# Turns between the stages of a two-layer streaming trunk, put in another order

## The chip, the core and the metric

One core of a Trainium2 chip runs the kernel. The metric is device microseconds (us) of one execution; three timed executions and one with the profiler stand below. TensorE (PE) multiplies, VectorE (DVE), ScalarE (ACT) and GpSimd (POOL) work on tiles of 128 partitions, and SyncE (SP) issues DMA transfers. TensorE runs at one of two levels, 2.4 or 1.2 GHz; the profile gives the granted clock as a share of the higher one.

## The reference, cut to what matters

Two layers on 1024 prompt rows and 128 sample rows, model width D = 1024, inner width E = 2048, all in float32.

```python
# mixer A: gated MLP over chunks of 128 rows
uv = gelu((xn @ w_in)[:, :2*E]); u, v = uv[:, :E], uv[:, E:]; z = (xn @ w_in)[:, 2*E:]
s = causal_mix(w_s, layernorm(v)) + b_s
x = x + (u * s * silu(z)) @ w_out
# mixer B: xLSTM memory, 4 heads of 512
xm, z = split(rmsnorm(x) @ b_w_in)            # each 2048 wide
xc = silu(causal_conv(xm))                    # 4 taps
q, k, v = blockdiag(xc, wq), blockdiag(xc, wk), blockdiag(xm, wv)
ig, fg = split(concat(q, k, v) @ w_gates + b_gates); lf = log_sigmoid(fg)
# running sums and maxima of ig, lf along the rows give weights exp(...)
C = decay * C + sum(w * k v^T);  h = (q C, intra-chunk part) / normaliser
x = x + ((layernorm(h) + skip * xc) * silu(z)) @ b_w_out
y = rmsnorm(x)                                # and C, n, m, conv of both row groups
```

## The kernel before, in words

**Numbers.** A float32 operand is split into a high part (ACT, a copy with rounding, line L89) and a low part (DVE, a subtraction, L90). A product is three matmuls into one PSUM sum: high by high, high by low, low by high (`mm3`). So before PE can start on an operand, ACT and then DVE have worked on it. PE's program order is the order of the code (class `Ordered`, L49); the order on the other engines is set by the framework's planner when the kernel is built, from its own estimate of times. SP's queue issues in order: an entry that waits holds up all behind it.

**Stages.** The 1152 rows are nine row tiles of 128, taken as three blocks of 384 (b). Mixer A first makes v, then a loop over 16 blocks of 128 features (f, L463 to L531) makes u, z and their product. It works on four quarters of 288 rows with seven products; their sums come out of PSUM by copies and additions (L499, L515 to L527, on tiles `c1`, `U2`, `e5`, `t`, `uq`), and two quarters each of `uq` and `c1` are written to o_d in DRAM, one step later, by the list `late` (L483).

The out-projection of A (L640 to L676) runs c (two halves of the output columns) by b by f: it loads a tile of o_d (`or`, L656), splits it (`os`) and multiplies. After each c and b `half_out` (L620) adds the residual and stores x1; with c = 1 it also sums squares on ACT (L632), and computes the normalised rows `xs` on DVE (L638), with the norm's weights `gB` (loaded at L594). `enter(n)` transposes row tile n on PE and splits it into `xh`, `xl`; most of these stand inside the next block, those of tiles 6 to 8 in mixer B's first steps (L832).

Mixer B's steps t (L820 to L843) make xm for a feature block and row block, the convolution, values, keys, and gate partials; q, k, v go to DRAM. Then 48 z blocks follow, each 24 matmuls of 128 by 384 with a Silu on ACT (L858) and a store (L859). `z_to(k)` (L865) emits z blocks until k are done. It is called between the parts of the gate stage (L885 to L1000): gate rows copied from PSUM (`rA`, L887), 48 small matmuls that add up the gate rows, then on tiles of 4 partitions by 1152 an Exp, a Ln, scans and three more Exps, and PE transposes of the results (`tpk`). After it the z blocks carry the state work by a plan (L1413 ff.): streams of 512 KB pieces of C in and out. Heads and the last projection follow.

Of the kernel before, what the change touches and what calls it, by code (L numbers as in the profile page):

```python
# [70 lines left out]
def trunk_kernel(ctx: ExitStack, tc: tile.TileContext, ins: dict, outs: list):  # L71
# [392 lines left out]
    for f in range(NF):  # L464
# [17 lines left out]
        def rows_of(o, q):  # L482
            late.append(lambda f=f: S.dma_start(out=o_d[f * P:(f + 1) * P, quarter(q)], in_=o))  # L483

        for i in range(7):
            rows_out_, late = late, []
            for p in range(2):
# [22 lines left out]
                elif i in (4, 5):  # L510
                    z, q = (e5[p], q1) if i == 4 else (U2[p], q0)
                    V.tensor_tensor(out=z, in0=acc, in1=z, op=ALU.add)
                    t = az.tile([P, QT], F32, name="t", bufs=3)
                    A.activation(out=t, in_=z, func=AF.Tanh, scale=0.5)
# [78 lines left out]
    wsm3 = kp_.tile([P, 3, NF, 4], F32, name="wsm3")  # L593
    gB = load_gB(ins["norm_g"][1], kp_, "gB")  # L594

# [24 lines left out]
    def half_out(n, c, po):  # L620
# [3 lines left out]
        S.dma_start(out=xv, in_=rows(n, ins["x_prompt"], ins["x_sample"])[:, cs])  # L624
        V.tensor_tensor(out=xv, in0=xv, in1=po, op=ALU.add)
        A.dma_start(out=x1_d[n][:, cs], in_=xv)
        if c == 0:
# [11 lines left out]
        xs_[n] = xs  # L639

    for c in range(2):
        for b in range(NB):
            po = [ps.tile([P, DH], F32, name="sm") for _ in range(3)]
            for f in range(NF):
# [7 lines left out]
                if c == 1 and b == 0 and f < 2:  # L652
                    fetch_wo(1, NF - 2 + f)
                    split_wo(1, NF - 2 + f)
                raw = ow.tile([P, BT], F32, name="or", bufs=6)
                S.dma_start(out=raw, in_=o_d[f * P:(f + 1) * P, b * BT:(b + 1) * BT])  # L656
                o = ow.tile([P, 2, BT], F32R, name="os")
# [9 lines left out]
            if c == 1 and b == 2:  # L667
                ow_stack.close()
                A_stack.close()
                rawp = ctx.enter_context(tc.tile_pool(name="rawp", bufs=4))  # L670
                wp = ctx.enter_context(tc.tile_pool(name="wp", bufs=6))
                w_first = load_w(b_w[:, :, 0:P])
            for j in range(3):
# [153 lines left out]
    for t, (f, b) in enumerate(steps):  # L827
        ft = feats[f]
        ft.inputs(b)
        if b == 0:  # L830
            ft.gate_weights()
        if (f, b) in ((1, 0), (1, 1)):  # L832
            for n in ((6,), (7, 8))[b]:
                enter(n)
        for j, part in ((t - 1, Feature.values), (t - 2, Feature.keys)):
            if j >= 0:
                part(feats[steps[j][0]], steps[j][1])
        if b == 1:
            ft.history()
        if t == 4 or (f > 1 and b == 1):  # L840
            if len(feats) < NF:
                feats.append(Feature(len(feats)))
            else:  # L843
                z_weights(0)
# [41 lines left out]
    for b in range(NB):  # L886
        V.tensor_copy(out=gsb[:, b * BT:(b + 1) * BT], in_=gp[32 * b:32 * b + 8])  # L887
    z_to(2)

# [23 lines left out]
    A.activation(out=t3, in_=t2, func=AF.Ln)  # L913
    z_to(4)
    lf = gt.tile([H, NTK], F32, name="rF")
# [5 lines left out]
    V.scalar_tensor_tensor(out=lf, in0=fg, scalar=0.0, in1=t3, op0=ALU.min, op1=ALU.subtract)  # L921
    z_to(6)

# [11 lines left out]

    z_to(7)

# [23 lines left out]
    V.tensor_tensor(out=cc_, in0=bb, in1=mt, op=ALU.subtract)  # L961
    z_to(8)
    wi_ = gt.tile([H, NTK], F32, name="rC")
# [12 lines left out]
    G.tensor_scalar(out=mt, in0=mt, scalar1=1e30, scalar2=1e-30, op0=ALU.min, op1=ALU.max)  # L976
    z_to(10)

# [430 lines left out]

    z_to(11)  # L1410
    open_head()
    z_to(12)
    heads[0].queries()  # L1413
    plan = {}
    plan.setdefault(13, []).append(heads[0].keys)
    plan.setdefault(14, []).append(heads[0].normaliser)
    first, rate = 14, (3 * NF - ZEND - 14) / (ZDEC - 1)
    for j in range(ZDEC):
# [169 lines left out]
```

## Time and profile before

| | |
|---|---|
| median of three timed runs | 1970.63 us (1969.28 to 1977.24) |
| profiled execution | 1961.52 us |
| its span on the core | 1959.8 us |
| mean granted clock of PE | 0.986 |
| PE busy | 1900.5 us, 11553 matmuls |
| DVE busy | 1270.3 us |
| ACT busy | 850.0 us |
| POOL busy | 621.4 us |

Busy times are of the span. PE is the engine that is almost always busy, so a time off the kernel must come from a stretch in which PE stands, or runs at the lower clock. Where the timeline says `[6.61 <-ACT os L89]`, the engine stood 6.61 us before this instruction, and what came last was the instruction named. PEclk in a window is 1.00 for the higher level throughout and 0.50 for the lower.

### The profile page before, as it was taken

The numbers are of one execution on the slowest core, as the hardware profiler recorded it, in microseconds if no ns is written. First come the engines' busy times: TensorE is split into PE (matmuls) and PEld (weight loads), VectorE is DVE, ScalarE is ACT, GpSimd is POOL, SyncE is SP. The second block draws the span as 40 slices with busy tenths as digits, with TensorE's granted clock in tenths as the row PEclk, the third lists the DMA queues.
The fourth block names the chain that finished last, engine by engine and source line by source line (L and its number), as shares of the span: only waits on it lengthen the run. The fifth ranks groups of instructions, "written<-read, shape, count | busy, mean of one in ns | idle before, by whom it ended". The sixth has DMA issues, their size and how long they took to land.

```text
span 1959.8 us, 32037 instructions
## 1 busy us (share of the span) xinstructions
PE 1900.5 (97%) x11553; PEld 1681.2 (86%) x11553; DVE 1270.3 (65%) x2522; ACT 850.0 (43%) x1727; POOL 621.4 (32%) x637
## 2 busy tenths in 40 slices
PE   7999999999998999989999989999999999999998
PEld 6888999999998788889999959888987787788887
DVE  5822477777776354477667635222498798898897
ACT  5422444444444243455555635112343344344454
POOL 3000244444441000035444401000145435345466
PEclk9999999999999999999999979999999999999999
DMA  6222333333334654335555554687998897775533
GB/s 213 92 92 77 106 98 103 103 103 99 103 98 163 200 170 142 113 99 154 161 162 156 167 152 143 207 259 235 282 306 264 267 284 243 261 239 177 154 122 129
DMA packets 345690, 328.21 MB, mean 167 GB/s; under 512 B 28164, under 2 KB 276948, under 8 KB 345532
## 3 DMA queue, kind: packets, MB, share of 16 engines
q1 hardware_dynamic: 288812, 261.03, 43.3%
q10 hardware_dynamic: 56720, 65.13, 10.6%
q8 instruction: 91, 1.49, 0.3%
q14 instruction: 67, 0.55, 0.1%
HBM read 203.07 MB, written 123.02 MB: 166 GB/s over the span
## 4 chain that ended last, share of the span: by engine, by line
PE 74%; DVE 13%; DMA 7%; ACT 2%; issue 2%; POOL 1%; SPq 1%; ACTq 0%; POOLq 0%; DVEq 0%
PE sm L58 74%; DVE Cst L1278 2%; DMA cw<-cw_d 2%; DVE c L1129 2%; DVE Cl L90 1%; DVE qT L1252 1%; DMA out<-c 1%; DVE raw L1361 1%; DVE bst L1318 1%; DMA c<-in_state_mlstm_C 1%; DMA vv<-vb_d 1%; DMA r<-in_a_w_in 0%; DVE dn L1324 0%; DVE x L1380 0%; DMA st_d<-w 0%
## 5 line engine op out<-in xcount | busy, mean ns | idle before, releaser
L58 PE MATMUL sm<-xh,w 128*128 128x384 f32 x1536 | 410.9, 341 | 4.3 <-DVE w L90 1.5
L58 PEld LDWEIGHTS sm<-xh,w 128*128 128x128 f32 x1536 | 281.5, 189 | 12.8 <-issue 8.2
L58 PE MATMUL sm<-xl,w 128*128 128x384 f32 x768 | 260.4, 339 | 1.1 <-DVE xl L90 1.1
L58 PE MATMUL sm<-Xh,w 128*128 128x288 f32 x1024 | 216.3, 298 | 4.6 <-ACT c L499 4.6
L58 PE MATMUL sm<-w,o 128*128 128x512 f32 x864 | 209.9, 398 | 2.9 <-ACT o L89 1.2
L58 PE MATMUL sm<-w,os 128*128 128x512 f32 x864 | 200.7, 393 | 6.6 <-ACT os L89 6.6
L58 PEld LDWEIGHTS sm<-w,os 128*128 128x128 f32 x864 | 162.9, 190 | 42.8 <-ACT os L89 9.1
L58 PEld LDWEIGHTS sm<-w,o 128*128 128x128 f32 x864 | 159.8, 188 | 41.1 <-ACT hn L1330 1.7
L58 PE MATMUL sm<-w,Xh 128*128 128x512 f32 x576 | 180.2, 394 | 1.8 <-DVE w L90 1.4
L58 PEld LDWEIGHTS sm<-Xh,w 128*128 128x128 f32 x1024 | 168.2, 189 | 5.2 <-ACT c L499 5.0
L90 DVE TENSOR_TENSOR w<-r,w 128x512 fp32r<-128x512 f32 x176 | 136.1, 779 | 50.3 <-ACT w L89 49.8
L58 PE MATMUL sm<-S,w 128*128 128x288 f32 x1152 | 163.8, 297 | 0.0
L90 DVE TENSOR_TENSOR w<-raw,w 128x1024 fp32r<-128x1024 f32 x44 | 56.4, 1281 | 156.8 <-ACT w L89 156.7
L58 PEld LDWEIGHTS sm<-S,w 128*128 128x128 f32 x1152 | 155.1, 188 | 0.8
L58 PE MATMUL sm<-Xl,w 128*128 128x288 f32 x512 | 151.4, 296 | 0.0
L58 PEld LDWEIGHTS sm<-xl,w 128*128 128x128 f32 x768 | 145.1, 189 | 1.3 <-DVE xl L90 1.3
L89 ACT CAST w<-r 128x512 fp32r<-128x512 f32 x176 | 107.3, 618 | 68.8 <-PE sm L58 29.3
L58 PEld LDWEIGHTS sm<-w,Xh 128*128 128x128 f32 x576 | 108.0, 189 | 25.3 <-DVE w L90 2.6
L58 PE MATMUL sm<-w,Xl 128*128 128x512 f32 x288 | 112.6, 391 | 0.0
L90 DVE TENSOR_TENSOR os<-or,os 128x384 fp32r<-128x384 f32 x96 | 53.0, 556 | 90.1 <-ACT os L89 90.1
L58 PE MATMUL sm<-va,k 128*128 128x258 f32 (+1 forms) x768 | 104.5, 286 | 3.4 <-DVE x L1380 1.7
L89 ACT CAST w<-raw 128x1024 fp32r<-128x1024 f32 (+1 forms) x56 | 55.2, 987 | 116.6 <-DMA raw<-in_b_w_in 91.2
(306 smaller groups left out, 3734.5 us busy)
## 6 DMA issues: line engine op xcount, KB each, us to landing
c<-in_state_mlstm_C SPq DMA_DIRECT2D x64, 512.0 KB
out<-c SPq DMA_DIRECT2D x64, 512.0 KB
r<-in_a_w_in SPq DMA_DIRECT2D x96, 256.0 KB
or<-o_d SPq DMA_DIRECT2D x96, 192.0 KB
raw<-in_b_w_in SPq DMA_DIRECT2D x32, 512.0 KB
qT<-q_d SPq DMA_DIRECT2D x40, 256.0 KB
vh<-v_d SPq DMA_DIRECT2D x48, 192.0 KB
vb_d<-st ACTq DMA_DIRECT2D x48, 192.0 KB
```

The lines of the kernel that those rows point to most:

```text
L58: ins = fn(*args, **kw)
L89: first = A.copy(out=hi, in_=src)
L90: (lo_eng or V).tensor_tensor(out=lo, in0=src, in1=f32(hi), op=ALU.subtract)
L1129: V.scalar_tensor_tensor(out=c0[:, cc], in0=c0[:, cc], scalar=decB[:, d.h, 8 + b:9 + b], in1=pc, op0=ALU.mult, op1=ALU.add)
L1252: V.tensor_tensor(out=u.g["qT"], in0=u.g["qT"], in1=u.g["cw"][:, 1:2].to_broadcast([P, DC, P]), op=ALU.mult)
L1278: V.scalar_tensor_tensor(out=Cst[:, c, a, :w], in0=Cst[:, c, a, :w], scalar=decB[:, h, n:n + 1], in1=pc, op0=ALU.mult, op1=ALU.add)
L1318: V.bn_stats(out=bst[:, a], in_=hn[:, a, :256])
L1361: V.scalar_tensor_tensor(out=og[:, c], in0=u.pT[:, c], scalar=colB[:, HNG, 4 * h + c:4 * h + c + 1], in1=g["sk"][:, c], op0=ALU.mult, op1= ...
```

## The change

Five edits. (1) The loop over f stores its last block's rows by POOL's queue instead of SP's, and `t` has four buffers instead of three. (2) The first four o_d loads of the out-projection are requested before its loops, and `gB` in its second block. (3) The split of mixer B's first weights is written out, and the add, store and square of row tile 6 (for the store and square 7 and 8 too) are held behind it. (4) The transposes of row tiles 6 to 8 come one step earlier in mixer B. (5) Four z blocks instead of two come ahead of the gate matmuls, each later `z_to` but one asks for one more, and the plan starts one block later.

```diff
--- before.py
+++ after.py
@@ -480,7 +480,7 @@
         al, be, ga, c1, U2, e5, uq, tz = ([None, None] for _ in range(8))
 
         def rows_of(o, q):
-            late.append(lambda f=f: S.dma_start(out=o_d[f * P:(f + 1) * P, quarter(q)], in_=o))
+            late.append(lambda f=f: (S if f + 1 < NF else G).dma_start(out=o_d[f * P:(f + 1) * P, quarter(q)], in_=o))
 
         for i in range(7):
             rows_out_, late = late, []
@@ -510,7 +510,7 @@
                 elif i in (4, 5):
                     z, q = (e5[p], q1) if i == 4 else (U2[p], q0)
                     V.tensor_tensor(out=z, in0=acc, in1=z, op=ALU.add)
-                    t = az.tile([P, QT], F32, name="t", bufs=3)
+                    t = az.tile([P, QT], F32, name="t", bufs=4)
                     A.activation(out=t, in_=z, func=AF.Tanh, scale=0.5)
                     V.scalar_tensor_tensor(out=t, in0=t, scalar=1.0, in1=z, op0=ALU.add, op1=ALU.mult)
                     if i == 4:
@@ -591,7 +591,7 @@
 
     gsum = kp_.tile([P, 2, NF, 8], F32, name="gsum")
     wsm3 = kp_.tile([P, 3, NF, 4], F32, name="wsm3")
-    gB = load_gB(ins["norm_g"][1], kp_, "gB")
+    gB = None
 
     def fold(i):
         t = kp_.tile([P, D], F32, name="xs", bufs=3)
@@ -622,8 +622,12 @@
         cs = slice(c * DH, (c + 1) * DH)
         xv = xa[:, n] if c == 0 else xap.tile([P, DH], F32, name="xb", bufs=3)
         S.dma_start(out=xv, in_=rows(n, ins["x_prompt"], ins["x_sample"])[:, cs])
-        V.tensor_tensor(out=xv, in0=xv, in1=po, op=ALU.add)
-        A.dma_start(out=x1_d[n][:, cs], in_=xv)
+        add = V.tensor_tensor(out=xv, in0=xv, in1=po, op=ALU.add)
+        if c == 1 and n == 6:
+            after(add, w_lo)
+        store = A.dma_start(out=x1_d[n][:, cs], in_=xv)
+        if c == 1 and n >= 6:
+            after(store, w_hi)
         if c == 0:
             return
         xs = kp_.tile([P, D], F32, name="xs", bufs=3)
@@ -638,8 +642,18 @@
             V.scalar_tensor_tensor(out=xs[:, hs], in0=src, scalar=r, in1=gB[:, hs], op0=ALU.mult, op1=ALU.mult)
         xs_[n] = xs
 
+    raws = {}
+
+    def fetch_o(b, f):
+        raw = raws[b, f] = ow.tile([P, BT], F32, name="or", bufs=6)
+        S.dma_start(out=raw, in_=o_d[f * P:(f + 1) * P, b * BT:(b + 1) * BT])
+
+    for f in range(4):
+        fetch_o(0, f)
     for c in range(2):
         for b in range(NB):
+            if c == 0 and b == 1:
+                gB = load_gB(ins["norm_g"][1], kp_, "gB")
             po = [ps.tile([P, DH], F32, name="sm") for _ in range(3)]
             for f in range(NF):
                 if c == 0 and b == 0 and f + 10 < NF:
@@ -652,8 +666,9 @@
                 if c == 1 and b == 0 and f < 2:
                     fetch_wo(1, NF - 2 + f)
                     split_wo(1, NF - 2 + f)
-                raw = ow.tile([P, BT], F32, name="or", bufs=6)
-                S.dma_start(out=raw, in_=o_d[f * P:(f + 1) * P, b * BT:(b + 1) * BT])
+                if (b, f) not in raws:
+                    fetch_o(b, f)
+                raw = raws.pop((b, f))
                 o = ow.tile([P, 2, BT], F32R, name="os")
                 split(o[:, 0], o[:, 1], raw)
                 w = wo[c, f]
@@ -669,7 +684,11 @@
                 A_stack.close()
                 rawp = ctx.enter_context(tc.tile_pool(name="rawp", bufs=4))
                 wp = ctx.enter_context(tc.tile_pool(name="wp", bufs=6))
-                w_first = load_w(b_w[:, :, 0:P])
+                raw, _ = fetch_w(b_w[:, :, 0:P])
+                w_first = wp.tile([P, 2, D], F32R, name="w")
+                w_hi = A.copy(out=w_first[:, 0], in_=raw)
+                w_lo = V.tensor_tensor(out=w_first[:, 1], in0=raw, in1=f32(w_first[:, 0]), op=ALU.subtract)
+                w_first = w_first.rearrange("p h (a b) -> p h a b", b=P)
             for j in range(3):
                 half_out(3 * b + j, c, po[j])
     xa_stack.close()
@@ -829,8 +848,8 @@
         ft.inputs(b)
         if b == 0:
             ft.gate_weights()
-        if (f, b) in ((1, 0), (1, 1)):
-            for n in ((6,), (7, 8))[b]:
+        if t in (1, 2):
+            for n in ((6,), (7, 8))[t - 1]:
                 enter(n)
         for j, part in ((t - 1, Feature.values), (t - 2, Feature.keys)):
             if j >= 0:
@@ -885,7 +904,7 @@
     gsb = gt.tile([8, NTK], F32, name="rA")
     for b in range(NB):
         V.tensor_copy(out=gsb[:, b * BT:(b + 1) * BT], in_=gp[32 * b:32 * b + 8])
-    z_to(2)
+    z_to(4)
 
 
     bgc = gt.tile([H, 2], F32, name="bgc")
@@ -911,7 +930,7 @@
     z_to(3)
     V.tensor_scalar(out=t2, in0=t1, scalar1=1.0, scalar2=None, op0=ALU.add)
     A.activation(out=t3, in_=t2, func=AF.Ln)
-    z_to(4)
+    z_to(5)
     lf = gt.tile([H, NTK], F32, name="rF")
 
     V.scalar_tensor_tensor(out=t1, in0=t2, scalar=1.0, in1=t1, op0=ALU.subtract, op1=ALU.subtract)
@@ -919,7 +938,7 @@
     V.tensor_tensor(out=t1, in0=t1, in1=t2, op=ALU.mult)
     V.tensor_tensor(out=t3, in0=t3, in1=t1, op=ALU.subtract)
     V.scalar_tensor_tensor(out=lf, in0=fg, scalar=0.0, in1=t3, op0=ALU.min, op1=ALU.subtract)
-    z_to(6)
+    z_to(7)
 
     keep = gt.tile([H, NTK], F32, name="rC")
     G.memset(keep, 1.0)
@@ -933,7 +952,7 @@
         sl = slice(1024 + b * SL, 1024 + (b + 1) * SL)
         V.tensor_tensor_scan(out=mt[:, sl], data0=lf[:, sl], data1=ig[:, sl], initial=m0T[:, b:b + 1], op0=ALU.add, op1=ALU.max)
 
-    z_to(7)
+    z_to(8)
 
     def ends(x):
         return (x[:, 0:1024].rearrange("p (n t) -> p n t", t=P)[:, :, P - 1],
@@ -959,7 +978,7 @@
 
     cc_ = gt.tile([H, NTK], F32, name="rF")
     V.tensor_tensor(out=cc_, in0=bb, in1=mt, op=ALU.subtract)
-    z_to(8)
+    z_to(9)
     wi_ = gt.tile([H, NTK], F32, name="rC")
     for (x, r), (y, _) in zip(parts16(cc_, mp16), parts16(wi_, mp16)):
         V.tensor_tensor(out=y, in0=x, in1=r, op=ALU.add)
@@ -974,7 +993,7 @@
     A.activation(out=ww, in_=ww, func=AF.Exp)
     A.activation(out=mt, in_=mt, func=AF.Exp, scale=-2.0)
     G.tensor_scalar(out=mt, in0=mt, scalar1=1e30, scalar2=1e-30, op0=ALU.min, op1=ALU.max)
-    z_to(10)
+    z_to(11)
 
     tok = const.tile([P, NT, 3, H], F32, name="tok")
     tpk = ps.tile([P, DH], F32, name="sm")[:, :NT * 3 * H].rearrange("p (n i h) -> p n i h", n=NT, i=3)
@@ -1407,14 +1426,14 @@
...
-    plan.setdefault(13, []).append(heads[0].keys)
-    plan.setdefault(14, []).append(heads[0].normaliser)
-    first, rate = 14, (3 * NF - ZEND - 14) / (ZDEC - 1)
+    plan.setdefault(14, []).append(heads[0].keys)
+    plan.setdefault(15, []).append(heads[0].normaliser)
+    first, rate = 15, (3 * NF - ZEND - 15) / (ZDEC - 1)
```

SP's queue at the turn from mixer A's loop to its out-projection, before: `r` are weights of the out-projection, `o_d<-` the last stores, `or` the row tiles.

```order
L483 DMA o_d_89<-uq_6439 128x288
L198 DMA gB_6669<-in_norm_g 128x1024
L483 DMA o_d_89<-c1_6346 128x288
L656 DMA or_6680<-o_d_89 128x384
L656 DMA or_6699<-o_d_89 128x384
L204 DMA r_6713<-in_a_w_out 128x512
L483 DMA o_d_89<-uq_6453 128x288
L656 DMA or_6718<-o_d_89 128x384
L204 DMA r_6732<-in_a_w_out 128x512
```

And now:

```order
L204 DMA r_6698<-in_a_w_out 128x512
L649 DMA or_6670<-o_d_89 128x384
L649 DMA or_6672<-o_d_89 128x384
L649 DMA or_6674<-o_d_89 128x384
L649 DMA or_6676<-o_d_89 128x384
L649 DMA or_6752<-o_d_89 128x384
L204 DMA r_6715<-in_a_w_out 128x512
L204 DMA r_6732<-in_a_w_out 128x512
L649 DMA or_6769<-o_d_89 128x384
L624 DMA xa_6669<-in_x_prompt 128x512 x3
L198 DMA gB_6932<-in_norm_g 128x1024
```

The stores of the last block are gone from this queue, four loads stand together at its head, and `gB` comes after the first x loads.

DVE at the turn to mixer B, before: `xb` are the residual adds of row tiles 6, 7, 8 (8390, 8404, 8418), `w_8387` the low part of the first weights, `xs` the normalised rows.

```order
L625 TENSOR_TENSOR xb_8418<-xb_8418,sm_8108 128x512
L634 TENSOR_TENSOR rr_8398<-ss2_8395 128x1
L166 TENSOR_SCALAR rr_8398<-rr_8398 128x1
L638 SCALAR_TENSOR_TENSOR xs_8394<-xa_6671,rr_8398,gB_6669 128x512
L90 TENSOR_TENSOR w_8387<-raw_8385,w_8387 128x1024
L638 SCALAR_TENSOR_TENSOR xs_8394<-xb_8390,rr_8398,gB_6669 128x512
L634 TENSOR_TENSOR rr_8412<-ss2_8409 128x1
```

And now:

```order
L625 TENSOR_TENSOR xb_8404<-xb_8404,sm_8107 128x512
L625 TENSOR_TENSOR xb_8418<-xb_8418,sm_8108 128x512
L690 TENSOR_TENSOR w_8387<-raw_8385,w_8387 128x1024
L625 TENSOR_TENSOR xb_8390<-xb_8390,sm_8106 128x512
L90 TENSOR_TENSOR w_8468<-raw_8466,w_8468 128x1024
L638 TENSOR_TENSOR rr_8398<-ss2_8395 128x1
L638 TENSOR_TENSOR rr_8412<-ss2_8409 128x1
L638 TENSOR_TENSOR rr_8426<-ss2_8423 128x1
```

The low part has moved ahead of the add of row tile 6 and of its first xs product.

ACT at the gate stage, before: `k_d` the store of the last keys, `rD`, `rA` the gate tiles (Exp at L910, Ln at L913), `st` a z block's Silu, `w` a high part of z weights.

```order
L798 DMA k_d3_101<-qk_12018 64x2x384
L910 ACT_TABLE_LOAD
L910 ACTIVATE rD_12111<-rD_12111 4x1152
L89 CAST w_12120<-raw_12118 128x1024
L913 ACT_TABLE_LOAD
L913 ACTIVATE rA_12113<-rE_12112 4x1152
L858 ACT_TABLE_LOAD
L858 ACTIVATE st_12108<-sm_12083 128x384
L859 DMA z_d0_110<-st_12108 128x384
```

And now (Exp at L929, Ln at L932, Silu at L877):

```order
L89 CAST w_12071<-raw_12069 128x1024
L877 ACTIVATE st_12066<-sm_12041 128x384
L878 DMA z_d0_110<-st_12066 128x384
L877 ACTIVATE st_12099<-sm_12074 128x384
L878 DMA z_d0_110<-st_12099 128x384
L929 ACT_TABLE_LOAD
L929 ACTIVATE rD_12144<-rD_12144 4x1152
L877 ACT_TABLE_LOAD
L877 ACTIVATE st_12176<-sm_12151 128x384
L932 ACT_TABLE_LOAD
L932 ACTIVATE rA_12146<-rE_12145 4x1152
```

Two Silus with their stores stand ahead of the Exp, and a third, with a table load of its own, between Exp and Ln.

## Rows read from the trace of the kernel before

**Rows 1.** The page, part 1: busy us (share) xinstructions of PE.

```profile
PE 1900.5 (97%) x11553; PEld 1681.2 (86%) x11553; DVE 1270.3 (65%) x2522; ACT 850.0 (43%) x1727; POOL 621.4 (32%) x637
```

**Rows 2.** Waits of PE: releaser, total us, times, longest us.

```profile
PE sm L58 <- DVE rA L887: 7.5, 1, 7.5
PE sm L58 <- ACT os L89: 6.6, 1, 6.6
PE sm L58 <- ACT c L499: 4.6, 2, 4.2
...
PE sm L58 <- DMA sk<-st_d: 2.4, 1, 2.4
```

**Rows 3.** Window of stage A's u/z loop: us, busy by engine, PEclk, DMA, GB/s.

```profile
400.00:449.00 49.00, 49.00 (x375) 48.76 (x374) 36.13 (x65) 23.64 (x56) 21.18 (x22) 1.00 0.35 103
```

**Rows 4.** Timeline at turn 1: start, us, engine line, [idle before, releaser].

```profile
622.51 0.29 PE L58 MATMUL sm<-Xh,w 128*128 128x288 f32 x1
...
622.84 0.33 SPq L198 DMA_DIRECT2D gB<-in_norm_g  x1
...
623.69 0.90 SPq L656 DMA_DIRECT2D or<-o_d  x2
...
627.01 0.44 DVE L527 SCALAR_TENSOR_TENSOR c<-c,t 128x288 f32<-128x288 f32 x1
...
628.85 1.05 ACT L89 CAST os<-or 128x384 fp32r<-128x384 f32 x2 [2.96 <-DMA or<-o_d]
...
629.41 0.79 PE L58 MATMUL sm<-w,os 128*128 128x512 f32 x1 [6.61 <-ACT os L89]
```

**Rows 5.** Chain that ended last: start, us, piece; a 192 KB load.

```profile
1236.95 3.27 DMA sk<-st_d
```

**Rows 6.** Window behind turn 1, columns as in Rows 3.

```profile
633.00:636.00 3.00, 3.00 (x13) 2.48 (x12) 1.66 (x5) 0.75 (x3) 0.00 (x0) 0.88 0.97 330
```

**Rows 7.** Timeline at turn 2 (PE, ACT, DVE, PE), columns as in Rows 4.

```profile
838.33 0.41 PE L58 MATMUL sm<-xh,w 128*128 128x384 f32 x1 [1.53 <-issue]
...
840.45 0.63 PE L58 MATMUL sm<-xh,w 128*128 128x384 f32 x2 [1.53 <-DVE w L90]
...
837.20 1.03 ACT L89 CAST w<-raw 128x1024 fp32r<-128x1024 f32 x1
...
839.18 1.22 DVE L90 TENSOR_TENSOR w<-raw,w 128x1024 fp32r<-128x1024 f32 x1
...
845.24 0.85 DVE L638 SCALAR_TENSOR_TENSOR xs<-xb,rr,gB 128x512 f32<-128x512 f32 x1
...
865.45 0.44 PE L58 MATMUL sm<-xh,w 128*128 128x384 f32 x1 [1.23 <-ACT xh L89]
866.95 0.45 PE L58 MATMUL sm<-xl,w 128*128 128x384 f32 x1 [1.06 <-DVE xl L90]
```

**Rows 8.** Timeline at turn 3 (PE, DVE, PE), columns as in Rows 4.

```profile
1154.57 1.44 PE L58 MATMUL sm<-rA,ident 8*4 8x384 f32 x2 [7.55 <-DVE rA L887]
...
1153.97 1.71 DVE L887 COPY rA<-sm 8x384 f32<-8x384 f32 x3 [11.75 <-DMA c<-in_state_mlstm_C]
...
1176.40 1.20 DVE L90 TENSOR_TENSOR w<-raw,w 128x1024 fp32r<-128x1024 f32 x1
...
1205.91 0.22 PE L58 MATMUL sm<-ident,rA 4*128 4x4 f32 x1
```

**Rows 9.** Windows at turn 3, columns as in Rows 3.

```profile
1147.00:1154.00 7.00, 0.02 (x1) 0.00 (x0) 0.03 (x1) 1.98 (x3) 0.00 (x0) 0.65 0.78 269
1170.00:1173.00 3.00, 3.00 (x12) 2.38 (x10) 1.84 (x2) 0.00 (x0) 0.00 (x0) 0.50 0.00 0
1176.00:1204.00 28.00, 28.00 (x161) 28.00 (x160) 19.09 (x29) 12.85 (x16) 4.04 (x5) 1.00 0.24 74
```

**Rows 10.** Chain that ended last, at turn 3: start, us, piece.

```profile
1154.57 16.52 PE sm L58 x48
...
1195.93 1.07 ACT rB L974
```

More of the change, by code (lines that the diff above doesn't have):

```diff
@@ L1408, in trunk_kernel @@
     stream_at = STREAMS
-    z_to(11)
+    z_to(12)
     open_head()
-    z_to(12)
+    z_to(13)
     heads[0].queries()
     plan = {}
-    plan.setdefault(13, []).append(heads[0].keys)
-    plan.setdefault(14, []).append(heads[0].normaliser)
-    first, rate = 14, (3 * NF - ZEND - 14) / (ZDEC - 1)
+    plan.setdefault(14, []).append(heads[0].keys)
+    plan.setdefault(15, []).append(heads[0].normaliser)
+    first, rate = 15, (3 * NF - ZEND - 15) / (ZDEC - 1)
     for j in range(ZDEC):
```

## The prediction

> **What bounds the kernel now.** The page comes first: TensorE (PE) is busy 1900.5 of 1959.8 us [rows 1], so only its idle time and its time at the lower clock can be won, some 60 us and what the clock adds. The list of what PE waited for comes next [rows 2]. The reader is to see that no wait repeats: four of the largest stand once or twice, and two of them at turns between stages (7.5 us for the gate rows, line L887; 6.6 us for the first split row tile, L89). The steady stretches are full: 49.00 of 49 us in stage A's u/z loop [rows 3]. So I read the turns one by one in the timeline, and beside them the granted clock by windows, since a long idle gap is followed by matmuls at the lower of TensorE's two levels, 1.2 instead of 2.4 GHz.
>
> All sums are made against the profiled execution, 1961.52 us (span 1959.8 and 1.7 around it). The median of the three timed runs is 1970.63, 9.1 above; I subtract the gain from the median.
>
> **Turn 1, stage A to its out-projection.** PE's last matmul starts at 622.51 and the next at 629.41, 6.61 us idle [rows 4]. The chain there is the first load of o_d (issued 623.69), its hi cast on ACT (628.85), PE. Ahead of that load on SP's queue stood the gB load at 622.84 and a store. The change puts the loads for four row tiles first, sends the last stores by POOL's queue and moves gB to the next block. gB waited for the same last matmul that frees the memory for the loads, so the first load goes out at about 622.84, 0.85 us sooner. From issue to cast it took 5.2 us behind gB's 512 KB; a 192 KB load alone took 3.27 [rows 5]. By the first the gain is 0.85, by the second 0.85 + 1.9 = 2.7. What is late next: the lo part, on DVE, which is in program order still behind the end of stage A (L527 at 627.01 to 627.45 [rows 4]); with the hi part at 626.7 PE would start and then wait about 0.8 for lo. PE also ran at half speed from 629.41 to about 633.7 (0.88 in the window from 633 [rows 6]), 2.1 us lost. A gap of some 4.5 us may or may not save this; fully saved the turn gives 4.8. Below nothing: stores on POOL, which has nothing to do there, land later than on SP, and the reader of block f=15 comes many us later; I allow -0.5. I take **1.7**, near the middle of 0.85 and 2.7.
>
> The Trainium skill ("DMA: Bandwidth & Descriptors", section "Issuing engines are not separate DMA queues") says that transfers share the same 16 engines whoever issues them, and that another issuer saves only the sequencer's time. By it the stores moved to POOL are worth some 0.3 us of SP each, and the turn would give 0.85 rather than 1.7.
>
> **The u/z loop.** The fourth t buffer lets tanh run without waiting for an older t, and the schedule answers by putting the multiplications of the second half ahead of the additions that free PSUM. In a steady step PE is never late [rows 3], so DVE's slack (36.13 busy of 49) hides it. Only the first step has a wait, 4.2 of the 4.6 us on L499 [rows 2]; one or two DVE instructions of 0.45 (as L527 in [rows 4]) move in front of the copy. I take **-0.3**, ends +1 and -1.5.
>
> **Turn 2, out-projection to mixer B.** PE waits 1.53 for hi of the first weights and 1.53 for lo [rows 7]. The first wait began at 836.80, the hi cast at 837.20 behind a square; lo started 0.95 after hi's end (837.20 + 1.03), behind an xs product on DVE. Now hi follows the last matmul directly (0.35 won) and lo follows hi directly (0.95): 1.3 sooner for the second wait, which is all that counts. The work put behind them (the row-6 add, its store and square) delays xs of row 6 by less than it is early: now it is wanted 16 matmuls earlier. The second part of it: the transposes of row tiles 6 to 8 move one step earlier, so their hi and lo copies (xh, xl) no longer end just before the matmuls that read them. The waits of 1.23 and 1.06 at 865.45 and 866.95 [rows 7] go if these copies come 2.3 us sooner; a step is more than that, but ACT and DVE work in order there with little idle time. I take 2.0 of 2.3. Together **3.3**, ends 1.2 and 3.8; less only if the transposes, wanted earlier, find their xs tile not ready: the last xs product ended at 846.1 [rows 7] and may end some 1.2 later behind the split, so about 1 is lost, and the low end is 0.2.
>
> **Turn 3, the gate stage.** This is the largest. PE idles 7.55 us until the gate rows are copied (1154.57), since the copy at 1153.97 waits for transfers [rows 8]. Then 48 small matmuls fill 16.5 us without a gap, at clock 0.50 all through (the window 1170 to 1173 stands for six such from 1155 on), and the first z block starts at 1171.0 at half speed; by 1176 the clock is 1.00 [rows 9, 10]. I count half speed to 1173.0, so 1.0 us lost. Cost of the turn: 7.55 + 16.45 + 1.0 = 25.0.
>
> Now two z blocks go ahead. A block is 24 matmuls; 161 take 28.0 us [rows 9], so 4.2 each. 8.4 covers 7.55 wholly, and as the copies wait for stores of the last keys, which are issued as before, they end at about 1155.6, when PE gets there. Blocks are only moved, so the wait is won in full. What the gate matmuls take hangs on the clock. At full speed 16.45 / 2 = 8.2; at half 16.45. They begin at full speed, since 100% z work precedes them. But the row shows that 16.5 us of them in a row never brought the clock back, while z matmuls did within 5: for the clock they count as little work. So I expect it to fall on the way, as it did in the gap from 1147 to 1154 (0.65 in the mean [rows 9], so full at first). Between 8.2 and 16.45 I take 13.2, above the middle, and for the z matmuls behind it 1.5 lost (1.0 here, 2.1 at turn 1). Cost after: 14.7; gain **10.3**. At the ends: 25.0 - 8.2 = 16.8, and 25.0 - 16.45 - 2.1 = 6.4.
>
> The Trainium skill ("TensorE: Matmul & The Clock Gate", section "What's actually happening") says that the clock follows how busy PE has been: idle lowers it, busy raises it. By the letter of it, gate matmuls without a gap keep the clock up, the stage costs 8.2, and the total comes to the first rival's. This trace speaks against that: PE is 100% busy for 16.5 us and the clock stays at 0.50.
>
> What is late next: the chain from the gate rows to the three tiles that PE transposes at 1205.91. Its end, rB's exponential, was done at 1197.00 [rows 8, 10], 26.0 after the gate matmuls' end at 1171.0, and PE came 34.9 after it: 8.9 us of cover. Now seven blocks instead of eight lie there: 34.9 - 4.2 = 30.7 or 1.0 less at full clock. The chain grows: a Silu now stands between Exp and Ln on ACT, with a table load and a wait for the fifth block's end (+0.9 to 1.7), and a lo split of 1.2 on DVE (as at 1176.40 [rows 8], there in a gap) stands inside. 26.0 + 2.9 = 28.9 at most 30: it just fits. I take **-0.5**, ends 0 and -4.
>
> The wait of 2.4 for st_d [rows 2] at the first state stream lies behind work that PE itself releases three blocks earlier, and all of it moves by one block alike; I take 0, ends +2.4 and -4 (the loads for it stand on SP behind the weights that the chain releases).
>
> **Sum.** 1.7 - 0.3 + 3.3 + 10.3 - 0.5 = 14.5. 1961.5 - 14.5 = 1947.0 as profiled, 1970.6 - 14.5 = **1956** timed. This forecast (the clock falls during the gate matmuls) has 0.56; its own range, with the terms half-way to their ends on one side or the other, 1951 to 1962.
>
> **Rivals.**
> 1. The clock stays up through the gate matmuls, and with it at turn 1: +6.5 and up to +2: 1948 to 1950. For it: z work at full speed right ahead. Against: the row of 0.50 above. 0.20.
> 2. The gate chain takes the place of the wait: ACT, switching tables between Silu, Exp and Ln, is late at the transposes, PE idles up to 4, the clock falls again (1.5 to 2), and st_d is 4 late: 14.5 - 9.5 = 5 left, 1965.6. For it: cover shrinks from 8.9 to about 1. Against: the sum above still fits. 0.15. Into the same place falls the case that the change does not do what it says: the copies of the gate rows wait for another transfer that starts later now, and the idle time only moves behind the two blocks; then turn 3 gives little and 5 are left: 0.03.
> 3. Slower: the u/z loop. If the new order on DVE makes PE wait for PSUM in each of 15 steps, as it waited once for 4.2, then x us per step cost 15x. From x = 1.0 the whole gain is gone; at 1.6 the time is 1956 + 24 = 1980. For it: the wait on L499 has this form. Against: PE 49.00 of 49, with 12.9 us of DVE idle in these 49 [rows 3]. 0.06.
>
> **Chances and range.** Faster or slower by over 0.5% means 9.9 us, about what a measurement of this kernel tells from no change. Faster: most of the forecast (0.47 of 0.56), all of rival 1 (0.20) and a little of 2 (0.04): 0.71. Slower: most of rival 3, 0.05. The same: 0.24. The range goes from 1948, rival 1, to 1967, rival 2 with 1.4 to spare.
>
> **What would show it.** Turn 1: the first o_d load as the first entry after 622.8 on SP, PE's gap there 4 to 6 us. Turn 2: waits on w of 1.5 and under 0.5, those at the xh and xl splits gone. Turn 3: no PE wait for L887, then the clock by windows over the gate matmuls: between 0.5 and 1.0 in the mean, and their stretch 11 to 14 us; 8.2 shows rival 1. A PE wait on rB or rE at the transposes shows rival 2; waits on L499 or L525 more than three times show rival 3. I am wrong altogether if the gate rows still end PE's longest wait, or if u/z windows fall under 48.5 of 49.

## The result, and the profile after

| | before | after |
|---|---|---|
| median of the first comparison | 1970.85 us | 1944.88 us |
| ratio, 95% interval | | 0.9882 [0.9858, 0.9906] |
| the same on two other chips | 1971.37 / 1972.33 | 1950.43 / 1949.41 |
| their ratios | | 0.9896 [0.9869, 0.9924] / 0.9882 [0.9865, 0.9898] |
| profiled execution | 1961.52 us | 1952.6 us |

The change takes 21 to 26 us off; 14.5 were forecast. The two profiled executions lie only 9 us apart, and the difference between them must not be read as the gain: executions of one program differ by some 10 us here. That of before is faster than all the other runs shown for it (1963.7 to 1980.8), that of after was the slowest of its first four (1944.2 to 1952.6). Much of this spread is in the lower clock. The mean clock was 0.984 in the middle of 23 runs of before and 0.992 in the middle of 14 of the changed kernel. (1 - clock) times the span bounds what the lower level costs: 31 us before, 16 after. So at most some 16 of the 21 to 26 us are clock, and 5 to 10 at least are idle time.

The page of after, part 1, and the core's line with its clock:

```profile
PE 1899.9 (97%) x11553; PEld 1684.0 (86%) x11553; DVE 1274.2 (65%) x2522; ACT 854.6 (44%) x1730; POOL 612.9 (31%) x641
```

```profile
core 0: 1950.9 us, clock 0.990
```

What PE waited for (releaser, total us, times, longest):

```profile
PE sm L58 <- ACT c L499: 5.6, 2, 4.7
PE sm L58 <- ACT os L89: 3.5, 1, 3.5
...
PE sm L58 <- DVE os L90: 1.0, 1, 1.0
...
PE sm L58 <- DVE w L690: 0.6, 1, 0.6
...
PE sm L58 <- ACT rB L993: 0.6, 1, 0.6
```

Against [rows 2], the wait for the gate rows (7.5) is gone, and so is that for st_d (2.4; it is 0.9 and 1.2 in two later profiles of the changed kernel); os has gone from 6.6 to 3.5 + 1.0, and a wait of 0.6 for rB is new. The one on L499 is 5.6 instead of 4.6.

Windows of after, columns as in [rows 3]: the u/z loop, turn 1, turn 2, two inside the gate matmuls, and one behind the transposes of their results.

```profile
400.00:449.00 49.00, 49.00 (x376) 48.76 (x375) 36.48 (x65) 24.00 (x56) 19.50 (x21) 1.00 0.35 103
633.00:637.00 4.00, 4.00 (x11) 3.10 (x11) 2.49 (x6) 1.75 (x3) 0.00 (x0) 0.53 1.06 382
841.00:845.00 4.00, 4.00 (x14) 4.00 (x15) 3.37 (x10) 1.59 (x6) 1.79 (x4) 0.57 0.20 72
1160.00:1163.00 3.00, 3.00 (x18) 1.08 (x18) 1.21 (x2) 0.79 (x1) 0.00 (x0) 1.00 0.43 160
1163.00:1166.00 3.00, 3.00 (x18) 1.08 (x18) 1.21 (x2) 0.00 (x0) 0.00 (x0) 1.00 0.99 260
1202.00:1206.00 4.00, 4.00 (x14) 4.00 (x14) 0.36 (x6) 0.00 (x0) 1.28 (x1) 0.50 0.91 297
```

The reader is to see three things: the u/z loop is as full as in [rows 3]; the gate matmuls run at 1.00, where 0.50 stood in [rows 9]; and the lower level turns up in places where the profile of before had none (841 to 845, 1202 to 1206). The first of these places is no effect of the change: the profile of turn 1's edits alone, whose turn 2 is that of before, has it too (0.50 from 842 to 846), and a second profile of the changed kernel has not (1.00 there).

**Turn 1**, timeline of after, to be held against [rows 4]:

```profile
625.36 0.29 PE L58 MATMUL sm<-Xh,w 128*128 128x288 f32 x1
625.68 2.25 SPq L649 DMA_DIRECT2D or<-o_d  x5
...
625.69 2.70 ACT L89 CAST w<-r 128x512 fp32r<-128x512 f32 x5 [0.19 <-PE sm L58]
...
626.93 3.08 DVE L90 TENSOR_TENSOR w<-r,w 128x512 fp32r<-128x512 f32 x5
...
628.64 0.91 ACT L89 CAST os<-or 128x384 fp32r<-128x384 f32 x2
...
629.19 0.73 PE L58 MATMUL sm<-w,os 128*128 128x512 f32 x2 [3.53 <-ACT os L89]
...
630.31 1.01 DVE L90 TENSOR_TENSOR os<-or,os 128x384 fp32r<-128x384 f32 x2
...
630.91 1.65 PE L58 MATMUL sm<-w,os 128*128 128x512 f32 x3 [0.99 <-DVE os L90]
```

The first o_d load is the first entry on SP after the last matmul, as forecast. Ahead of the os cast ACT makes five weight casts, which end 2.7 us after that matmul, and DVE five low parts. ACT's casts stood there before too, but then the os cast waited 2.96 us more for the load [rows 4]:

```profile
622.84 2.70 ACT L89 CAST w<-r 128x512 fp32r<-128x512 f32 x5 [0.56 <-PE sm L58]
```

Now ACT works without a pause from these casts to the os cast, and the low part of os stands behind DVE's five. PE stands 3.53 + 0.99 instead of 6.61, 2.1 less. The lower clock takes some of it back. By windows it was 0.50 from 629 to 633 and 0.88 from 633 to 636 before, and is 0.73 from 629 to 631, 0.50 from 631 to 633 and 0.53 from 633 to 637 now. By an estimate from these, some 3 us of PE's work are lost to it instead of 2.1, and about 1.2 us of the gain are left in this profile.

**Turn 2**, PE in the timeline, against [rows 7]:

```profile
839.78 0.41 PE L58 MATMUL sm<-xh,w 128*128 128x384 f32 x1 [1.18 <-issue]
...
841.00 0.62 PE L58 MATMUL sm<-xh,w 128*128 128x384 f32 x2 [0.62 <-DVE w L690]
...
878.28 0.81 PE L58 MATMUL sm<-xc,gsum 128*8 128x384 f32 x2 [0.82 <-ACT xc L779]
```

The `issue` wait ahead of the first row is 1.18 instead of 1.53, the one for the low part 0.62 instead of 1.53, and those at the splits xh and xl are not there. The wait of 0.82 in the last row is new: it is 0.8 to 1.1 in five profiles with edit 4 (this one, two more of the changed kernel, turn 2's edits alone, edits 1 to 4), and it is not in that of before.

**Turn 3**, PE and then DVE in the timeline, against [rows 8]:

```profile
1158.52 0.80 PE L58 MATMUL sm<-rA,ident 8*4 8x384 f32 x2
...
1166.67 0.82 PE L58 MATMUL sm<-ident,gtok 128*4 128x128 f32 x6
1167.41 0.44 PE L58 MATMUL sm<-xh,w 128*128 128x384 f32 x1
...
1197.97 0.22 PE L58 MATMUL sm<-ident,rB 4*128 4x4 f32 x1 [0.57 <-ACT rB L993]
```

```profile
1154.47 1.71 DVE L906 COPY rA<-sm 8x384 f32<-8x384 f32 x3 [9.11 <-DMA m0T<-in_state_mlstm_m]
```

The copies of the gate rows come sooner against the last keys: their first starts 4.3 us behind the last keys' matmuls (1154.47 against 1150.16), where it started 6.95 behind them (1153.97 against 1147.02). The last store of keys and the loads of C (512 KB each) stand in another order; before, and then after:

```profile
1147.99 6.17 SPq L1111 DMA_DIRECT2D c<-in_state_mlstm_C  x4
1148.45 0.61 ACTq L798 DMA_DIRECT2D k_d<-qk  x1
```

```profile
1151.54 0.62 ACTq L817 DMA_DIRECT2D k_d<-qk  x1
1153.48 1.41 SPq L1130 DMA_DIRECT2D c<-in_state_mlstm_C  x3
```

The first copy waits for this store (the profile of edits 1 to 4 names it), and the store now starts ahead of the loads. In the chains of two other kernels below it took 5.59 us with the loads of C ahead of it (edits 1 to 4) and 2.74 with them behind it (the wait taken away). That it is the loads that slow it is argued from this, not tested by itself. So some 5 us were left to cover instead of 7.55, and the two z blocks (8.4) run over them. The 48 gate matmuls take from 1158.52 to 1167.41, 8.9 us instead of 16.5. At the transposes PE waits 0.57 for rB.

### The profile page after: what moved, and what is told of

Read it like the earlier page. It is cut to its first block, busy times and chain, and to the rows that moved or that the text cites. A ratio compares the mean times of both kernels' runs of the same rounds, so it can differ in the third digit from the quotient of the medians.

```text
span 1950.9 us, 32048 instructions
## 1 busy us (share of the span) xinstructions
PE 1899.9 (97%) x11553; PEld 1684.0 (86%) x11553; DVE 1274.2 (65%) x2522; ACT 854.6 (44%) x1730; POOL 612.9 (31%) x641
## 4 chain that ended last, share of the span: by engine, by line
PE 74%; DVE 12%; DMA 7%; ACT 3%; issue 2%; POOL 2%; SPq 0%; ACTq 0%; POOLq 0%; DVEq 0%
PE sm L58 74%; DVE Cst L1297 2%; DMA cw<-cw_d 2%; DVE c L1148 2%; DMA raw<-in_b_w_in 1%; DVE Cl L90 1%; DMA raw<-in_b_w_out 1%; DVE qT L1271 1%; DMA out<-c 1%; DVE raw L1380 1%; DVE bst L1337 1%; DMA x<-in_x_prompt 1%; DMA vv<-vb_d 1%; DVE xc L777 0%; ACT w L89 0%
## 5 line engine op out<-in xcount | busy, mean ns | idle before, releaser
L58 PEld LDWEIGHTS sm<-va,k 128*128 128x128 f32 x768 | 98.4, 192 | 7.6 <-DVE x L1399 4.3
```

The lines of the kernel that those rows point to most:

```text
L58: ins = fn(*args, **kw)
```

## Experiments

Each was compared with the kernel before on its own chip. Differences are of medians.

**Edit 5 alone**, and **edits 1 to 4 without it**: the parts of the diff, nothing else.

> The kernel before with the two more z blocks ahead of the gate matmuls and the shifted z counts alone (edit 5). Theory A (the clock stays at its higher level through the gate matmuls when they start at it): no PE wait for the gate rows, the 48 gate matmuls in 8 to 9 us with the granted clock at 1.00, 15 to 18 us off, 1953 to 1956. Rival B (the clock falls during them, as forecast): 12 to 14 us for them, 9 to 11 off, about 1961; the rest of the change's 26 us would then be in the other two turns.

> The changed kernel without edit 5 (two z blocks ahead of the gate matmuls, the z counts and the plan as before), edits 1 to 4 in. Theory A (the parts add up, and edit 5 is worth 18 to 19): 1.4 + 3.7 and something for the t buffers off, 4 to 8 us, with the gate wait of 7.5 and 16.5 us of gate matmuls at 0.50 as before. Rival B (the parts help each other): under 3 or over 10 us off.

Edit 5 alone: 1954.16, ratio 0.9906 [0.9891, 0.9922], 18.6 off. In its profile there is no wait for the gate rows and the clock does not fall at them: theory A. Edits 1 to 4: 1970.86, 0.9994 [0.9975, 1.0013], 0.5 off. That is under 3, as rival B had it, and not the 4 to 8 of theory A; the interval, from 2.6 us slower to 4.9 faster, leaves room for either. The changed kernel beside it took 1950.43, so edit 5 on top of the others gave 20.4. Edit 5 is nearly all that can be measured.

**Turn 1, turn 2 and the t buffers, each alone.**

> The kernel before with the first four o_d loads ahead, gB in the second block and the last stores on POOL (edits 1 without the fourth t buffer, and 2). Theory A: PE's gap at this turn 6.6 -> 4.5, 2 to 3 us off, 1968. Rival B (this turn holds what edit 5 does not): 8 to 10 us off, 1962, with the clock never falling at 627.

> The kernel before with the split of mixer B's first weights written out and the transposes of row tiles 6 to 8 one step earlier (edits 3 and 4). Theory A: waits of 1.5 + 1.5 + 1.2 + 1.1 shrink to about 2 in all, 3 to 4 us off, 1967. Rival B: 6 or more off, with a stretch at the lower clock gone that the one profile of before does not show.

> The kernel before with four t buffers in the u/z loop instead of three, alone. Theory A: within 1 us of the kernel before (PE 49.00 of 49 us in the loop either way; the one wait on L499 4 to 5). Rival B: 3 us or more faster, by a wait in the loop that differs between executions and that the fourth buffer takes away.

Turn 1: 1970.15, 0.9993 [0.9979, 1.0007]. Turn 2: 1968.59, 0.9981 [0.9967, 0.9995]. The t buffers: 1971.50, 0.9992 [0.9974, 1.0009]. Rival B is out for turn 1. For turn 2 (6 or more) and the t buffers (3 or more) the upper ends of the intervals, 6.5 and 5.1, still touch it. Only turn 2's gain is clear of nothing, 1 to 6.5 us. That the edits together gave 0.5, at most 4.9 by the interval, says that more than about 5 us isn't in them.

**The changed kernel with the gate matmuls doubled.**

```diff
-            T.matmul(pg[:H, :BT], ident[:8, 4 * i:4 * i + 4], gsb[...], start=True, stop=False)
+            for _ in range(2):
+                T.matmul(pg[:H, :BT], ident[:8, 4 * i:4 * i + 4], gsb[...], start=True, stop=False)
...
```

> The changed kernel with each of the 12 groups of gate matmuls done twice (the second overwrites the first), so about 18 us of them instead of 8.9. Theory A (at the upper level the gate matmuls keep it, however little they do): all of it at granted clock 1.00, about 17.8 us, 9 slower than the changed kernel. Rival B (they count as too little, and the 8.9 us were only over before the clock fell): the clock falls within the stretch, 22 to 30 us, 13 to 21 slower.

1959.81 in two runs, ratio 0.9928 [0.9909, 0.9947]; against the changed kernel's 1949 to 1950 on other chips some 9 to 10 slower (6 to 9 by the ratios to the kernel before). Windows over the doubled matmuls:

```profile
1159.00:1168.00 9.00, 9.00 (x49) 3.14 (x48) 1.41 (x4) 1.73 (x2) 0.00 (x0) 1.00 0.90 284
1168.00:1176.00 8.00, 8.00 (x44) 2.71 (x43) 1.67 (x3) 0.00 (x0) 0.00 (x0) 1.00 0.12 32
```

17 us of them at 1.00. Rival B is out: it was not that they ended just in time. The same matmuls that did not bring the clock back in 16.5 us [rows 9, 10] hold it when it is up.

**The kernel before with the wait for the stores taken away**, the z blocks where they were.

```diff
-    gsb = gt.tile([8, NTK], F32, name="rA")
+    gsb = wp.tile([P, 2, D], F32, name="w").rearrange("p a d -> p (a d)")[:8, :NTK]
```

> The kernel before, with the gate rows copied into a slot of the weights' pool that no store of keys still reads, so the wait of 7.5 us ahead of the gate matmuls goes without any z block put there. Theory A (what counts is the level at which the gate matmuls start): PE's gap falls to 1 or 2 us, the gate matmuls run at 1.00 in some 9 us as long as DVE empties their sums, and the turn gives most of what two z blocks ahead give, 10 to 16 us. Rival B (z blocks ahead are needed): the gate matmuls still run at 0.50 in 16.5 us, and about 6 us are gained.

1957.25 in two runs, 0.9915 [0.9896, 0.9933], 15.7 off. PE in the timeline:

```profile
1149.03 0.86 PE L58 MATMUL sm<-xc,bd 128*128 128x384 f32 x4
1149.83 0.80 PE L58 MATMUL sm<-w,ident 8*4 8x384 f32 x2
...
1157.97 0.82 PE L58 MATMUL sm<-ident,gtok 128*4 128x128 f32 x6
```

No gap, no block in between, and 9 us at the upper level. So what the z blocks did was to fill the gap; another way of closing it does the same. The turn's cost went from 25.0 to 8.9, 16.1 by the trace of before. What edit 5's 18.6 has beyond this is later on; in this kernel PE still waits for st_d:

```profile
PE sm L58 <- DMA sk<-st_d: 4.7, 1, 4.7
```

**One z block ahead instead of two** (the kernel before with `z_to(3)` in place of `z_to(2)`).

> The kernel before with one z block more ahead of the gate matmuls instead of two, and no other count changed. PE then waits about 7.5 - 4.2 = 3.3 us for the gate rows. Theory A (the level at which the gate matmuls start is kept): if the clock is still at 1.00 when they start, 9 us for them and some 12 to 14 off; if it falls in the gap, 16.5 us and 4 to 5 off; nothing between. Rival B (they wear the clock down in proportion): a stretch between 10 and 15 us.

1967.65, 0.9968 [0.9943, 0.9994], its runs spread from 1956 to 1973. In the profiled one (1960.09) the rows came earlier than reckoned (here too the loads of C were issued behind the last store of keys, 1151.74 against 1149.71), and PE stood only 0.82:

```profile
1153.36 0.80 PE L58 MATMUL sm<-rA,ident 8*4 8x384 f32 x2 [0.82 <-DVE rA L887]
1154.09 0.82 PE L58 MATMUL sm<-ident,gtok 128*4 128x128 f32 x6
...
1155.58 0.97 PE L58 MATMUL sm<-ident,gtok 128*4 128x128 f32 x6
1156.47 1.44 PE L58 MATMUL sm<-rA,ident 8*4 8x384 f32 x2
```

The stretch is 14.1 us, inside rival B's 10 to 15, but not by its mechanism: the matmuls start at the upper level (0.80 a group), 2.8 us into them the clock falls (1.44 a group), and 17 us of the same matmuls without a gap had worn nothing down. Theory A, as I had put it, does not hold either: the level at the start is not simply kept. Left over was that the gap beside them decides.

**The changed kernel with a gap put back**: the copies of the gate rows done three times over, so that the matmuls are late behind the same two z blocks.

```diff
-    for b in range(NB):
-        V.tensor_copy(out=gsb[:, b * BT:(b + 1) * BT], in_=gp[32 * b:32 * b + 8])
+    for _ in range(3):
+        for b in range(NB):
+            V.tensor_copy(out=gsb[:, b * BT:(b + 1) * BT], in_=gp[32 * b:32 * b + 8])
```

> The changed kernel with the copies of the gate rows done three times over, so that the gate matmuls start late and PE idles some 1 to 3 us ahead of them, behind the same two z blocks. Theory A (a gap next to the gate matmuls takes the clock down although the matmuls alone keep it): the clock falls some 2 to 5 us into the gate matmuls and they take 13 to 15 us; 6 to 10 slower than the changed kernel. Rival B (in the kernel with one block ahead it fell for another reason, and what counts is the level at the start alone): they run at 1.00 in 9 us, and only the gap is lost, 2 to 4.

1958.47 in two runs against 1949.41 for the changed kernel beside it, 9.1 slower.

```profile
1157.99 0.80 PE L58 MATMUL sm<-rA,ident 8*4 8x384 f32 x2 [2.61 <-DVE rA L907]
...
1159.47 0.80 PE L58 MATMUL sm<-rA,ident 8*4 8x384 f32 x2
1160.20 1.30 PE L58 MATMUL sm<-ident,gtok 128*4 128x128 f32 x6
1161.44 1.44 PE L58 MATMUL sm<-rA,ident 8*4 8x384 f32 x2
...
1171.03 1.44 PE L58 MATMUL sm<-ident,gtok 128*4 128x128 f32 x6
```

A gap of 2.61, and 2.4 us into the matmuls the clock falls; they end near 1172.4, 14.4 us after their start. 2.6 of gap and 5.5 of clock make 8.1 of the 9.1. Theory A here: without a gap beside them the gate matmuls hold the upper level, with one they do not. All 18 kept profiles agree. In the eleven with no gap ahead of these matmuls they run at the upper level throughout. In five with a gap of 7.1 to 7.9 us they run at the lower one throughout, and in the two above they fall to it.

**A third z block ahead of the transposes of the gate results** (the changed kernel, `z_to(12)` for `z_to(11)` there, and the plan one block later).

> The changed kernel with one more z block ahead of the transposes of the gate results (and the plan one block later). Theory A: the wait of 0.6 us on rB and the stretch at the lower clock from 1200 on (3.4 to 6.8 us of it, 1.7 to 3.4 lost) go, and 1 to 4 us are won, 1941 to 1944, if the wait for st_d stays away. Rival B: the clock falls there by the small matmuls alone, or the state streams lose what is won: within 1 us of the changed kernel.

1964.00, 0.995 [0.9933, 0.9966]: some 14 us worse than the changed kernel's 1949 to 1950 on other chips (11 to 13 by the ratios), worse than either theory allowed. The chain that ended last (start, us, piece), and PE in the timeline:

```profile
1194.69 1.81 DMA cw_d<-rC
...
1196.55 0.37 SPq L1056
...
1198.11 7.33 DMA raw<-vb_d
```

```profile
1228.19 1.88 PE L58 MATMUL sm<-raw,blk 128*8 128x512 f32 x2 [7.63 <-ACT raw L1101]
```

The weights c of the state part (`cw_d`) come from the gate chain. Their load (L1056) waits for it on SP, and the loads for the first head (`raw` from k_d and vb_d) stand behind it in the same queue; they land late, ACT's order carries it on, and PE stands 7.63 and then runs at the lower level for some 6 us (0.50 from 1228 to 1232, 0.69 to 1236). In the changed kernel the same two loads are issued 24 us ahead of that of c:

```profile
1174.46 0.37 SPq L1080 DMA_DIRECT2D raw<-k_d  x1
1174.87 0.50 SPq L1081 DMA_DIRECT2D raw<-vb_d  x1
1198.74 0.36 SPq L1056 DMA_DIRECT2D cw<-cw_d  x1
```

So no cover is missing behind the transposes: from them to this matmul PE works some 21 us in both. What differs is the order that the planner gave SP's queue. That this order alone costs the gap was not tested. In the kernel before the two loads stood behind that of c as well, and PE did not wait; there the load of c was issued 8.1 us ahead of the transposes (1197.81 against 1205.91), here 2.6. The gap is also the smaller part of the loss: from this matmul to the end the profile takes 736.9 us, with one z block fewer than in the 728.6 of after, and what is lost there was not followed up.

**Turn 1 with the row tiles split first** (the changed kernel; casts and low parts of weight tiles 10 to 13 held behind those of the row tile).

```diff
-                    split_wo(0, f + 10)
...
-                split(o[:, 0], o[:, 1], raw)
+                os_hi = A.copy(out=o[:, 0], in_=raw)
+                os_lo = V.tensor_tensor(out=o[:, 1], in0=raw, in1=f32(o[:, 0]), op=ALU.subtract)
+                if c == 0 and b == 0 and f + 10 < NF:
+                    wn = w2.tile([P, 2, DH], F32R, name="w")
+                    after(A.copy(out=wn[:, 0], in_=wo[0, f + 10]), os_hi)
...
```

> The changed kernel with the first four row tiles of o_d split ahead of the weight tiles 10 to 13 on ACT and DVE. Theory A (turn 1 is now bound by ACT and DVE, which split four weight tiles first): PE's gap of 3.5 + 1.0 falls to 2 to 3 and 2 to 3 us are won. Rival B (the load itself lands no sooner than 628.5): within 1 us of the changed kernel.

The os cast on ACT, and PE:

```profile
626.42 0.51 ACT L672 CAST os<-or 128x384 fp32r<-128x384 f32 x1 [1.62 <-DMA or<-o_d]
```

```profile
626.98 13.21 PE L58 MATMUL sm<-w,os 128*128 128x512 f32 x50 [3.19 <-ACT os L672]
```

PE's gap is 3.19 in one piece instead of 3.53 and 0.99; ACT now waits for the load. 1951.01, ratio 0.9882 [0.9863, 0.9900], is no different from the changed kernel's: a gain of some 1 us is not to be seen, and theory A's 2 to 3 are not shown.

**A version with eight blocks behind the gate matmuls** (the changed kernel with the gate rows in the weights' pool, as above, and `z_to(3)` for `z_to(4)`), run twice, once also with the row tiles first, and the changed kernel beside it.

> The changed kernel with the gate rows in a slot of the weights' pool (they wait for no store of keys) and one z block instead of two ahead of the gate matmuls, so eight instead of seven lie between them and the transposes of their results. Theory A (the chain of gate scalars is what is late next): the wait of 0.6 on rB and the stretch at the lower clock behind it go, and the loads of the state part come 4 us sooner against PE: 2 to 5 us below the changed kernel. Rival B (that clock stretch is brought on by the small transposes themselves, and the chain has cover enough): within 1 us of the changed kernel.

> The version with the gate rows in a slot of the weights' pool and one z block ahead of the gate matmuls, once more: 2 to 5 us below the changed kernel if its first result (1945.9 against 1950.4) was no chance; within 1 us of it if it was.

> That version with the first four row tiles of o_d split ahead of the weight tiles 10 to 13 as well. Theory A (turn 1 is bound by ACT and DVE): 1 to 3 us below the version without it. Rival B: within 1 us of it.

> The changed kernel itself again, on the chip of the runs beside it: 22 to 28 us below the kernel before.

> The changed kernel once more, on the chip of the runs beside it: 20 to 26 us below the kernel before.

The version: 1945.89, 0.9869 [0.9838, 0.9900], and 1947.77, 0.9875 [0.9858, 0.9892]; with the row tiles first 1947.98, 0.9874 [0.9859, 0.9890]. The changed kernel beside them: 1950.43 and 1949.41, which is 20.9 and 22.9 below the kernel before; for the first, 22 to 28 had been expected. The wait for rB is gone in both profiles of the version; the stretch at the lower clock behind it is gone in the first and there in the second (0.57 from 1197 to 1200). The medians are 4.5 and 1.6 lower than the changed kernel's, and the intervals overlap: perhaps better, not shown. The row tiles first add nothing to it (1947.98 against 1947.77), as rival B had it.

## Why the prediction was wrong

**The step that failed** is in turn 3: "for the clock they count as little work. So I expect it to fall on the way ... Between 8.2 and 16.45 I take 13.2 ... and for the z matmuls behind it 1.5 lost". Measured: 8.9 for the gate matmuls and nothing lost behind them (1.00 from 1167 to 1197); the turn costs 8.9 and not 14.7, and gives 16.1 and not 10.3. With that in its place the sum is 20.3 off, 1950. It was rival 1, with a chance of 0.20, at 1948 to 1950, and the two later comparisons of the changed kernel (1950.4, 1949.4) come out at its upper end. The first one, 1944.9, lies 3 us under the whole range; the 26.0 us that it shows (18.5 to 28.0 by its interval) are not explained beyond these 20. The row of 0.50 over 16.5 us was read rightly as far as it goes: these matmuls do not raise the clock. What does not follow is that they let it fall. The doubled stretch shows that they don't, the two kernels with a gap show what does. The rule of the Trainium skill ("TensorE: Matmul & The Clock Gate", section "What's actually happening") that busy keeps the clock up gave the right time here; its other half, that busy raises it, is not what [rows 9] show, and in the two kernels with a gap the clock fell while PE was busy again. I set the second half against the first.

**The wait ahead of them**: right that it is covered; PE did not wait. The copies did not come as reckoned. They were to end 8.6 us behind the last keys (1155.6 against 1147.0), as before, and ended 6.0 behind them (1156.2 against 1150.2). This was luck for the change, and more than it needed: 8.4 us of z blocks would have covered 7.55 too.

**What is late next**: right in place and size as far as PE's wait goes (0.57 on rB, taken as 0.5); the chain took 30.5 us from the end of the gate matmuls, where 28.9 to 30 was reckoned. Not counted was the clock: PE ran at the lower level behind the transposes (0.50 from 1200 to 1206, 0.80 to 1208), 3.4 us lost in this profile and 1.7 in two later ones. Whether the wait brings it on is open: the stretch is in all six kept profiles with this wait, and in four of twelve without it. Against it stands the wait for st_d, 2.4 before with some 1.7 of clock behind it (0.82 from 1240 to 1242, 0.66 to 1246), and none in the profile of after. I had taken 0 for it; why it shrank I did not test. The two about cancel.

Yet edit 5 alone gave 18.6 (15.4 to 21.5 by its interval), where the turn itself gave 16.1. The profiles place the rest behind the first state matmul (`raw,blk`). From there to the end it is 733 to 743 us, 739 in the mean, in five profiles with the wait for the gate rows as it was (before, turn 1, turn 2, the t buffers, edits 1 to 4). It is 729 to 732, 730 in the mean, in four with edit 5 (alone, and three of the changed kernel), which have one z block (4.2) less there: some 5 us, those of st_d among them. 16.1, less 2.3 to 4.0 at the transposes, and these 5 make 17 to 19. What made that part shorter is open.

**Rival 2** happened in part: ACT is late at the transposes by 0.57 and the clock falls behind them, but PE does not idle 4 us. The experiment with one block more ahead of the transposes lost some 14 us. Part of it went through SP's queue, which I had named ("the loads for it stand on SP behind the weights that the chain releases") and priced at 4; the rest was not followed up.

**Turn 1**: the mechanism right, the gain 2.1 of idle time against 1.7 in the sum. The half speed behind it stayed and cost some 0.9 more (0.53 in the window from 633), and the next late thing was ACT's and DVE's weight splits, which the prediction had not looked at, rather than the end of stage A. In the timing the turn can't be told from nothing. The load of [rows 5], 3.27 us, did not run alone: a load of 512 KB was issued 0.4 behind it. No run sets the stores by POOL's queue apart.

**Turn 2**: right. 5.6 us of waits became 1.8 and a new one of 0.8, and alone it measured 4.2 in the median (1 to 6.5) against 3.3.

**The u/z loop**: no loss by step, 49.00 of 49 as before, so rival 3 is out. Its one wait on L499 is longer. The longest is 4.4 to 6.6 us in twelve profiles with four t buffers, 5.8 in the mean, and 3.7 to 5.4 in six with three, 4.5 in the mean: some 1.3 are lost, where 0.3 was taken. Together with the clock at turn 1 this may be why edits 1 to 4 gave next to nothing; it was not tested.

**The base of the sum**: the profiled run of before, 9 us below the median, had fewer stretches at the lower level than the others (0.986 against 0.984). The gain was taken from the median, so this did no harm; a reader who compares the two profiles alone would see 9 us in place of 23. That no wait of PE repeats was misread: the longest entry of that list, which [rows 2] do not show, is 8.3 us in seven waits (`x`, L1380). Nothing in the sum rests on it.

## What to carry to other kernels

Close the small gap next to a stretch of small matmuls before moving anything large: 0.8 and 2.6 us of idle time each cost some 5 us of clock here, more than themselves. When blocks are moved to cover one wait, read the built kernel's queues again, since the planner may put other loads first: here one block more, meant to give cover, came with two loads behind a waiting one, and the kernel was 14 us slower. And where executions of one kernel differ by 10 us, read from a profile where time goes, and from many runs how much.

## What was not expected of the hardware

The same 48 matmuls (8 rows by 4 columns, and 128 by 4) ran at 0.50 for 16.5 us when the clock was down at their start, at 1.00 for 8.9 us, and doubled for 17 us, when it was up and PE came straight from other matmuls, and fell from 1.00 to 0.50 after 2.8 and 2.4 us when 0.82 or 2.61 us of idle time lay ahead of them.
